# Two-layer decoder trunk on one core: causal masks, priorities of head operations, and the place of two slab sums

## The chip, the cores and the metric

The kernel runs on one core of a Trainium2 chip. The core has four computing engines with a queue of instructions each: TensorE (PE; its weight loads are shown apart as PEld), VectorE (DVE), ScalarE (ACT) and GpSimd (POOL). SyncE (SP) issues the transfers. Each engine works through its queue in order; an instruction that has to wait for another engine, by a semaphore, holds everything behind it in the queue. The metric is the device time of one execution in microseconds, lower is better.

## The reference

The input is 256 tokens of width 2048, a memory of 256 tokens, and the weights. There are two layers, all in float32:

```python
for i in range(DEPTH):
    if i == 1: sk1, sk2, sv = shared_kv(x, kv_norm, w_kv, k_norm, cos, sin)
    u = rms_norm(x, mix_norm[i]) @ w_in[i]
    # layer 0: causal pooling of 4 channel groups, then a linear map per group
    # layer 1: 12 difference heads, a = softmax(q1 k1) - lam * softmax(q2 k2), causal,
    #          o = a @ v, then an RMS norm per head
    # both: 4 memory heads, softmax(q k_mem) @ v_mem, not causal
    x = x + concat([token_out, mem_out]) @ w_out[i]
    x = x + squared_relu_mlp(rms_norm(x, ffn_norm[i]), w_ff1[i], w_ff2[i])
```

The causal mask adds -1e30 to the scores of later keys ahead of the softmax.

## The kernel before

**Precision and weights.** Each float32 weight is split into a high part in TensorE's fast float32 format and a low part. ScalarE makes the high part (`hi`, L157), VectorE the low part (`lo`, L158), both into a ring of six slots of 512 columns. Transfers by SP bring the weights in 512 KB pieces (`raw`, and `slab` for the part described last). One slot feeds six to twelve matmuls, and the splits run three slots ahead of use (class `Feed`).

**Stages of layer 1.** The stage that the change touches is layer 1's attention. `b_tile` makes the query projections in three column blocks c = 0, 1, 2, of four heads each. After each block the queries are normed, rotated and turned (`query_rows`, `rope`, `query_scale`, `turn_queries`). Then four tiles `mq1` make the memory queries (`c_tile`), and then output tiles `wo` follow (`out_tiles`): the first three tiles are begun with the channels that are ready (eight, then four, then the last four), and tiles 3 to 15 are done one by one. Heads are not computed where they stand in the program: `at(lag, fn)` puts their parts into a table, and each completed weight slot (`tick`) runs the parts that are due. So the parts of heads are spread between the large matmuls.

**A difference head** (`diff_head`, L1175 and after) has four parts. `scores`: matmuls of both maps for the second half of the queries (`s1`, 256 keys) and for the first half (`s0`, 128 keys); the mask; a maximum over keys (L1207); four exponentials with sums (L1211); reciprocal and combination. `turn`: three transposes (`dt`, L1226) and a copy. `pv`: three output matmuls (`do`, L1232 to L1234), their squares (L1242), a reciprocal root from ScalarE and VectorE steps (`rsqrt_cols`), and two scalings into `osb` (L1250). `back`: two transposes (`o_t`, L1255) and the split into `cat1` (`split_gain`).

Two ways of masking exist. With `by_pe` false VectorE adds the mask to the scores (L1202, L1203). With `by_pe` true TensorE adds it as a bf16 matmul of the identity with the mask (L1189, L1193), and in `pv` the output is first copied out of its bank into `osb` (L1237), from which squares and scalings then read. The caller passes `c == 2`: heads 8 to 11 take the second way.

**A memory head** (`mem_head`) has scores (`ms`, L573), a maximum (L575), exponentials (L579), a reciprocal and two multiplications (L584, L586); four transposes (`mt`, L592) and a copy (L595); two output products (`mo`, L600) with a copy and a subtraction out of the bank (L601, L602). `mem_query` makes the norm of its query beforehand (`st_mq`, L553).

**PSUM.** The pool has tags with few buffers, one bank each: `mm` three (tiles `mq1`, `wo`), `s` two (`s1`, `s0`, `ms` in turn), `t` one (`dt`, `mt`, `tq`), `o` one (`do`, `mo`), `st` one (`o_t`, `st_mq`). A tile's first matmul waits until every reader of the buffer's earlier tile is done.

**What sets the order.** The program only states the work. A scheduler puts each engine's instructions in order by a priority (the earlier in the program, the higher) and by when it expects them to be ready. That order is then fixed.

**Slabs.** In the feed-forward part, half of the second weight goes through a 2x2 block scheme with seven products, whose weights are sums of blocks ("slabs"). `Feed._prepare` with job "K" makes the first two sums on VectorE (L182 and L183). `out_tiles` adds each finished output tile to the residual in two steps (`resid_add`, L638 and L639); a `wo` tile waits until the tile three before it has been added.

Of the kernel before, what the change touches and what calls it, by code (L numbers as in the profile page):

```python
# [10 lines left out]
F32 = mybir.dt.float32  # L11
# [94 lines left out]
class Feed:  # L106


    def __init__(self, nc, wst, wpool, rows, plan, dry):
        self.nc, self.wst, self.wpool, self.rows = nc, wst, wpool, rows  # L110
        self.plan, self.dry = plan, dry
        self.pos = 0
        self.slab_no = 0
        self.lp = self.pp = 0
        self.raw = {}
        self.split = {}
        self.t1 = None
        if not dry:
            self.hi = wpool.tile([P, SLOTS * 512], F32R, name="hi_ring")
            self.lo = wpool.tile([P, SLOTS * 512], F32R, name="lo_ring")  # L120
            self.busy = [False] * SLOTS
            self.at = 0
# [39 lines left out]
    def _prepare(self, p):  # L162
        sub, add = self.nc.vector.tensor_sub, self.nc.vector.tensor_add
        self.load(self.plan.need[p] + 1 + LOADS)
        if p[0] == "N":
            r = ("N", p[1] // 2)
            c = p[1] % 2 * 512
            if not self._split(p, self.raw[r][:, c : c + 512], 1):
                return False
            if c:  # L170
                del self.raw[r]
            return True
        ra, rb = self.raw[("S", p[1], 0)], self.raw.get(("S", p[1], 1))
        t1 = self.t1[1 if p[1] % 32 > 28 else p[1] % 2]

        def both():
            t2 = rb[:, 0:512].unsqueeze(1).to_broadcast([P, 2, 512])
            two = ra.rearrange("p (a c) -> p a c", a=2)
            sub(two, t2, two)

        if p[0] in "KL":
            add(t1, ra[:, 0:512], rb[:, 0:512])  # L182
            sub(rb[:, 0:512], t1, rb[:, 512:1024])  # L183
            if p[0] == "L":
                both()
# [77 lines left out]
def program(ctx, tc, plan, dry, xT, memT, par, lam, cst, wst, yT):  # L263
# [8 lines left out]
    feed = Feed(nc, wst, wp, tp, plan, dry)  # L272

    acc = {}

# [12 lines left out]
    def flush():  # L288
        while pend:
            tick()  # L290


    def vt(name):
        return tp.tile([P, T], F32, tag="v", bufs=6, name=name)
# [246 lines left out]
    def mem_query(src, gq, cols):  # L541
# [1 line left out]

        q = vt("mq")
        sq = vt("mq_sq")
        nc.scalar.activation(q, src, AF.Copy, scale=gq)
        nc.scalar.activation(sq, src, AF.Square)
        y = tp.tile([P, 2], F32, tag="m2", bufs=12, name="mq_y")

        def stats():  # L550
            st = stat("st_mq")
            for t in range(2):
                nc.tensor.matmul(  # L553
                    st[:, 2 * t : 2 * t + 2], sq[:, t * P : t * P + P], ones_h,
                    start=True, stop=True,
                )
            v2 = tp.tile([P, 2], F32, tag="m2", bufs=12, name="mq_v")
            nc.vector.tensor_mul(v2, st[:, 0:4].rearrange("p (a b) -> p a b", b=2)[:, :, 0], cols[1])
            nc.vector.tensor_scalar_add(v2, v2, EPS)
            rsqrt_cols(y, v2)  # L560
            nc.vector.tensor_mul(y, y, cols[0])

        at(2, stats)
        return q, y
# [1 line left out]
    def mem_head(q, y, k, v, e, pT, out, lag, pv_lag=6):  # L566
# [3 lines left out]
        def scores():  # L570
            s = pp.tile([P, 2, T], F32, tag="s", bufs=2, name="ms")
            for t in range(2):
                nc.tensor.matmul(s[:, t, :], q[:, t * P : t * P + P], k, start=True, stop=True)  # L573
            m = tp.tile([P, 2], F32, tag="m2", bufs=12, name="mm_max")
            nc.vector.tensor_reduce(out=m, in_=s, axis=AX.X, op=ALU.max, negate=True)  # L575
            nc.vector.tensor_mul(m, m, y)
            z = tp.tile([P, 2], F32, tag="m2", bufs=12, name="mm_sum")
            for t in range(2):
                nc.scalar.activation(  # L579
                    e[:, t, :], s[:, t, :], AF.Exp, bias=m[:, t : t + 1], scale=y[:, t : t + 1],  # L580
                    accum_out=z[:, t : t + 1],
                )
            zr = tp.tile([P, 2], F32, tag="m2", bufs=12, name="mm_rec")
            nc.vector.reciprocal(zr, z)  # L584
            for t in range(2):
                nc.vector.tensor_scalar_mul(e[:, t, :], e[:, t, :], zr[:, t : t + 1])  # L586

        def turn():
            t4 = pp.tile([P, 2, T], F32, tag="t", bufs=1, name="mt")
            for mb in range(2):  # L590
                for t in range(2):
                    nc.tensor.transpose(  # L592
                        t4[:, mb, t * P : t * P + P], e[:, t, mb * P : mb * P + P], ident
                    )
            nc.scalar.copy(pT, t4)  # L595

        def pv():
            o = pp.tile([P, T], F32, tag="o", bufs=1, name="mo")
            for mb in range(2):
                nc.tensor.matmul(o, v(mb), pT[:, mb, :], start=mb == 0, stop=mb == 1)  # L600
            nc.scalar.copy(out[:, 0:T], o)  # L601
            nc.vector.tensor_sub(out[:, T : 2 * T], o, out[:, 0:T].bitcast(F32))  # L602

        at(lag, scores)
        at(lag + 4, turn)
# [30 lines left out]

    def resid_add(ps, n):
        nc.vector.tensor_add(resid[:, n, :], resid[:, n, :], ps[:, 0:T])  # L638
        nc.vector.tensor_add(resid[:, n, :], resid[:, n, :], ps[:, T : 2 * T])  # L639

    def resid_done(n, splits, square=True):
        for dst, g in splits:
# [385 lines left out]
    def out_tiles(l, cat, lead, ks, fx, between):  # L1028
# [6 lines left out]
        for n in range(NK):  # L1035
# [3 lines left out]
            else:  # L1039
                ps = mmt("wo")  # L1040
                a_part(ps, "w_out", l, n, sum(lead, []) + ks, cat)
            resid_add(ps, n)
            resid_done(n, [(fx, G_FFN + 16 * l)])

    group_u(3)
# [109 lines left out]
    def turn_queries(rows, i, pair):  # L1155
# [4 lines left out]
                    t4[:, c, t * P : t * P + P], rows[:, t, (i + c) * P : (i + c) * P + P], ident  # L1160
                )
        for g, r in enumerate((slice(0, 64), slice(64, 128))):
            nc.scalar.activation(pair[g][r], t4[r], AF.Copy, scale=qcol[r])


    gsub = cp.tile([P, 1], F32, name="gsub")
# [8 lines left out]
    def diff_head(h, q, y, lag, pv_lag, back_lag, by_pe):  # L1175
# [6 lines left out]
        def scores():  # L1182
# [11 lines left out]
            else:  # L1194
# [9 lines left out]
            mx = tp.tile([P, 2, 2], F32, tag="m4", bufs=6, name="mx")  # L1204
            z = tp.tile([P, 2, 2], F32, tag="m4", bufs=6, name="z")
            for t, s in ((1, s1), (0, s0)):
                nc.vector.tensor_reduce(out=mx[:, t, :], in_=s, axis=AX.X, op=ALU.max, negate=True)  # L1207
            nc.vector.tensor_mul(mx, mx, yh)
            for t, s, e in ((1, s1, e1), (0, s0, e0)):
                for m in range(2):  # L1210
                    nc.scalar.activation(  # L1211
                        e[:, m, :], s[:, m, :], AF.Exp, bias=mx[:, t, m : m + 1],
                        scale=yh[:, t, m : m + 1], accum_out=z[:, t, m : m + 1],
                    )

            zr = tp.tile([P, 2], F32, tag="m2", bufs=12, name="zr")
            nc.vector.reciprocal(zr, z[:, :, 1])
            stt(zr, zr, nlam, z[:, :, 0], ALU.mult, ALU.mult)
            stt(ez, z[:, :, 0], EPS, z[:, :, 0], ALU.mult, ALU.mult)
            for t, e, dst in ((1, e1, a[:, P : P + T]), (0, e0, a[:, 0:P])):  # L1220
                stt(dst, e[:, 1, :], zr[:, t : t + 1], e[:, 0, :], ALU.mult, ALU.add)

        def turn():
            t3 = pp.tile([P, 384], F32, tag="t", bufs=1, name="dt")
            for i in range(3):
                nc.tensor.transpose(t3[:, i * P : i * P + P], a[:, i * P : i * P + P], ident)  # L1226
            nc.scalar.copy(aT, t3)

        def pv():
            o = pp.tile([P, 2, P], F32, tag="o", bufs=1, name="do")  # L1230
# [1 line left out]
            nc.tensor.matmul(o[:, 0, :], aT[:, 0:P], vv[:, 0, hs], start=True, stop=True)  # L1232
            nc.tensor.matmul(o[:, 1, :], aT[:, P:T], vv[:, 0, hs], start=True, stop=False)
            nc.tensor.matmul(o[:, 1, :], aT[:, T : T + P], vv[:, 1, hs], start=False, stop=True)  # L1234
            osb = vt("osb").rearrange("p (a b) -> p a b", a=2)
            if by_pe:
                nc.vector.tensor_copy(osb, o)  # L1237
                o = osb
            ss = tp.tile([P, 2], F32, tag="m2", bufs=12, name="o_ss")
            junk = vt("o_sq")  # L1240
            for t in range(2):
                nc.scalar.activation(  # L1242
                    junk[:, t * P : t * P + P], o[:, t, :], AF.Square, accum_out=ss[:, t : t + 1]
                )
            v = tp.tile([P, 2], F32, tag="m2", bufs=12, name="o_v")
            stt(v, ss, 1.0 / P, ez, ALU.mult, ALU.add)
            yo = tp.tile([P, 2], F32, tag="m2", bufs=12, name="o_y")
            rsqrt_cols(yo, v)
            for t in range(2):
                nc.vector.tensor_scalar_mul(osb[:, t, :], o[:, t, :], yo[:, t : t + 1])  # L1250

            def back():
                f = pp.tile([P, T], F32, tag="st", bufs=1, name="o_t")
                for t in range(2):
                    nc.tensor.transpose(f[:, t * P : t * P + P], osb[:, t, :], ident)  # L1255
                split_gain(cat1[:, h, :], f, gsub)

            at(back_lag, back)

# [4 lines left out]
    for c in range(3):  # L1264
        ps = pair_of_banks(0, "q1")
        b_tile(ps, "w_in_q", 1, c, x_mx)
        rows, v = query_rows(ps, c1, 64)
        rope(rows, qtab)
        y = query_scale(v, c1)
        for i in range(2):  # L1270
            j = 2 * c + i
            q = qb[j % 3]
# [104 lines left out]
```

## Time and profile before

| What | Value |
| --- | --- |
| median of three runs | 2045.28 us (2045.19 to 2045.52) |
| the profiled execution | 2044.93 us |
| its span | 2043.1 us |
| PE busy | 2037.2 us |
| DVE busy | 1716.2 us |
| ACT busy | 1349.8 us |
| POOL busy | 51.9 us |
| DMA | 390.75 MB, mean 191 GB/s |

The span runs from the first to the last instruction of the program; the execution's own time is 1.8 us longer. The granted TensorE clock is 1.0 throughout. Matmuls are pipelined, so that the duration of one (0.39 us for 512 columns) is longer than the distance to the next (0.23 us): a gap shows as a distance above the usual one, or as idle time in brackets. In the timeline, "x2" merges neighbours of one line; in the list of waits the columns are the total, the number, and the longest, in us.

### The profile page before, as it was taken

The page shows a single profiled execution, that of the slowest core. Times are in us where ns is not written, and L with a number is a line of the kernel's source. Part 1 is how long each engine was busy: PE and PEld are TensorE (multiplying, and loading weights), DVE is VectorE, ACT ScalarE, POOL GpSimd, SP SyncE. Part 2 cuts the span into 40 slices and gives each one's busy share as a digit, 9 for nine tenths or more (in the row PEclk, how much of TensorE's full clock was granted, in tenths as well). Part 3 has the DMA queues.
Part 4 walks back from the last instruction along what each step waited for, and adds up shares of the span by engine and source line. Part 5 has one row for each costly group of instructions (what it writes and reads, how often), then busy time and mean ns, then how long its engine had stood idle before and what let it go on. Part 6 is the DMA issues. An engine that isn't in the chain of part 4 may idle for free.

```text
span 2043.1 us, 32257 instructions
## 1 busy us (share of the span) xinstructions
PE 2037.2 (100%) x11060; PEld 1755.3 (86%) x11060; DVE 1716.2 (84%) x3215; ACT 1349.8 (66%) x2505; POOL 51.9 (3%) x67
## 2 busy tenths in 40 slices
PE   9999999999999999999999999999999999999999
PEld 8888888888888888888888888888888888888888
DVE  8888889889879978999766687889879978988997
ACT  7765566666666756768665697566657666666764
POOL 0001200000000000000000000310000000000000
PEclk9999999999999999999999999999999999999999
DMA  9556556555555555655565543656555555565564
GB/s 314 178 181 190 188 174 206 197 196 197 186 201 202 189 207 191 207 169 182 194 228 186 170 140 103 196 166 207 196 196 205 186 196 196 186 210 195 196 209 135
DMA packets 110470, 390.75 MB, mean 191 GB/s; under 512 B 12256, under 2 KB 14944, under 8 KB 110304
## 3 DMA queue, kind: packets, MB, share of 16 engines
q1 hardware_dynamic: 110160, 388.59, 57.1%
q8 instruction: 86, 1.41, 0.3%
q14 instruction: 80, 0.66, 0.1%
q10 hardware_dynamic: 144, 0.10, 0.0%
HBM read 386.54 MB, written 2.10 MB: 190 GB/s over the span
## 4 chain that ended last, share of the span: by engine, by line
PE 99%; ACT 1%; DVE 1%; issue 0%
PE x_bank L391 33%; PE x_bank L393 16%; PE wo L391 6%; PE p L746 5%; PE p L747 5%; PE p L748 5%; PE wo L393 3%; PE u L391 2%; PE ff L391 2%; PE u L393 1%; PE k L417 1%; PE k L419 1%; PE v L417 1%; PE k L418 1%; PE v L419 1%; PE v L418 1%
## 5 line engine op out<-in xcount | busy, mean ns | idle before, releaser
L157 ACT CAST hi_ring<-raw 128x512 fp32r<-128x512 f32 x1193 | 736.7, 620 | 529.5 <-PE x_bank L391 308.0
L158 DVE TENSOR_TENSOR lo_ring<-raw,hi_ring 128x512 fp32r<-128x512 f32 x1193 | 817.2, 695 | 206.7 <-ACT hi_ring L157 165.5
L391 PE MATMUL x_bank<-fx,hi_ring 128*128 128x512 f32 x1920 | 602.1, 395 | 0.0
L393 PEld LDWEIGHTS x_bank<-fx,lo_ring 128*128 128x128 f32 x1920 | 361.0, 188 | 83.6
L393 PE MATMUL x_bank<-fx,lo_ring 128*128 128x256 f32 x1920 | 377.4, 278 | 0.0
L391 PEld LDWEIGHTS x_bank<-fx,hi_ring 128*128 128x128 f32 x1920 | 301.4, 189 | 9.3
L391 PE MATMUL x_bank<-z,hi_ring 128*128 128x512 f32 x960 | 301.1, 395 | 0.0
L158 DVE TENSOR_TENSOR lo_ring<-slab,hi_ring 128x1024 fp32r<-128x1024 f32 x188 | 230.1, 1224 | 54.3 <-ACT hi_ring L157 53.6
L157 ACT CAST hi_ring<-slab 128x1024 fp32r<-128x1024 f32 x188 | 196.9, 1047 | 73.1 <-PE x_bank L391 36.2
L393 PEld LDWEIGHTS x_bank<-z,lo_ring 128*128 128x128 f32 x960 | 180.5, 188 | 41.7
L393 PE MATMUL x_bank<-z,lo_ring 128*128 128x256 f32 x960 | 188.8, 278 | 0.0
L391 PE MATMUL wo<-cat,hi_ring 128*128 128x512 f32 x512 | 162.5, 398 | 0.5 <-DVE resid L639 0.5
L391 PEld LDWEIGHTS x_bank<-z,hi_ring 128*128 128x128 f32 x960 | 151.9, 189 | 6.5 <-ACT room L672 0.4
L393 PEld LDWEIGHTS wo<-cat,lo_ring 128*128 128x128 f32 x512 | 95.9, 188 | 21.7
L672 ACT COPY room<-x_bank 128x512 f32<-128x512 f32 x180 | 104.9, 583 | 2.0 <-PE x_bank L393 2.0
L393 PE MATMUL wo<-cat,lo_ring 128*128 128x256 f32 x512 | 101.4, 279 | 0.0
L746 PE MATMUL p<-hi_ring,sit 128*128 128x512 f32 x256 | 100.5, 393 | 0.0
L747 PE MATMUL p<-hi_ring,sit 128*128 128x512 f32 x256 | 100.2, 391 | 0.0
L748 PE MATMUL p<-lo_ring,sit 128*128 128x512 f32 x256 | 99.7, 389 | 0.0
L391 PEld LDWEIGHTS wo<-cat,hi_ring 128*128 128x128 f32 x512 | 79.1, 189 | 2.2 <-PE wo L393 0.9
L717 ACT ACTIVATE room<-room 128x256 f32<-128x256 f32 x128 | 53.2, 416 | 39.1 <-DVE room L300 39.1
L746 PE MATMUL p<-hi_ring,z 128*128 128x512 f32 x192 | 75.2, 392 | 0.0
(313 smaller groups left out, 3102.3 us busy)
## 6 DMA issues: line engine op xcount, KB each, us to landing
raw<-in_w SPq DMA_DIRECT2D x595, 512.0 KB, 4.0
slab<-in_w SPq DMA_DIRECT2D x124, 512.0 KB, 3.3
resid<-in_x SPq DMA_DIRECT2D x8, 256.0 KB, 5.9
room<-in_w SPq DMA_DIRECT2D x4, 512.0 KB, 4.2
memraw<-in_mem SPq DMA_DIRECT2D x4, 512.0 KB, 3.6
out_y<-resid SPq DMA_DIRECT2D x16, 128.0 KB, 1.8
memraw<-in_mem SPq DMA_DIRECT2D x7, 256.0 KB, 6.3
raw<-in_w SPq DMA_DIRECT2D x3, 256.0 KB, 3.5
```

The lines of the kernel that those rows point to most:

```text
L157: self.nc.scalar.copy(hi, src)
L158: self.nc.vector.tensor_sub(lo, src, hi.bitcast(F32))
L391: nc.tensor.matmul(ps, hi, xs[:, k, :], start=first and c == 0, stop=False)
L393: nc.tensor.matmul(ps[:, T : 2 * T], lo, xs[:, k, 0:T], start=False, stop=last and c == len(ks) - 1,)
L417: nc.tensor.matmul(ps[t], xl, hi, start=k == 0, stop=False)
L418: nc.tensor.matmul(ps[t], xh, hi, start=False, stop=False)
L419: nc.tensor.matmul(ps[t], xh, lo, start=False, stop=k == NK - 1)
L672: nc.scalar.copy(x, ps)
L717: at(3, lambda: nc.scalar.activation(stage[i % 8], y[:, 0:T], AF.Square))
L746: nc.tensor.matmul(ps, a[1], hi, start=first, stop=False)
L747: nc.tensor.matmul(ps, a[0], hi, start=False, stop=False)
L748: nc.tensor.matmul(ps, a[0], lo, start=False, stop=last)
```

## The change

Three things. First, `diff_head` is called with `by_pe` False for all heads: heads 8 to 11 now take VectorE's masks, and the output is no longer copied out of its bank. Second, most ScalarE and VectorE operations of the heads, of `mem_query`, of the queries' norm and turning, stand in `with early():`, which is the scheduler's context of high priority. Third, an ordering edge, without a semaphore, for the scheduler alone: the first slab sum after output tile 2 (the third of the 16) is put behind that tile's second residual addition; the program sets it once in each layer.

```diff
-            add(t1, ra[:, 0:512], rb[:, 0:512])
+            one = add(t1, ra[:, 0:512], rb[:, 0:512])
+            if self.gate:
+                self.tc.add_manual_dep(
+                    one.ins, self.gate,
+                    mybir.DependencyInfo(
+                        mybir.DependencyClass.NoSync, mybir.DependencyReason.SCHED_ONLY
+                    ),
+                )
+                self.gate = None
...
+    def early():
+        return tc.high_priority()
...
-        nc.scalar.activation(q, src, AF.Copy, scale=gq)
-        nc.scalar.activation(sq, src, AF.Square)
+        with early():
+            nc.scalar.activation(q, src, AF.Copy, scale=gq)
+            nc.scalar.activation(sq, src, AF.Square)
...
-            nc.scalar.copy(out[:, 0:T], o)
-            nc.vector.tensor_sub(out[:, T : 2 * T], o, out[:, 0:T].bitcast(F32))
+            with early():
+                nc.scalar.copy(out[:, 0:T], o)
+                nc.vector.tensor_sub(out[:, T : 2 * T], o, out[:, 0:T].bitcast(F32))
...
-            resid_add(ps, n)
+            done = resid_add(ps, n)
+            if n == 2 and not dry:
+                feed.gate = done.ins.name
...
-                nc.vector.tensor_add(s1[:, :, P:T], s1[:, :, P:T], mask)
-                nc.vector.tensor_add(s0, s0, mask)
+                with early():
+                    nc.vector.tensor_add(s1[:, :, P:T], s1[:, :, P:T], mask)
+                    nc.vector.tensor_add(s0, s0, mask)
...
-                    2 * j + g, q[g], y, *((6 + 4 * h, 8, 4 if c == 0 else 3) if c < 2 else (6 + 2 * h, 6, 3)), c == 2
+                    2 * j + g, q[g], y, *((6 + 4 * h, 8, 4 if c == 0 else 3) if c < 2 else (6 + 2 * h, 6, 3)), False
```

In the same way the following stand in the context of high priority: the rest of `scores`, the copy in `turn` and all of `pv` and `back` of a difference head but the matmuls; the statistics of `mem_query`; softmax and copies of a memory head; `query_rows`, `rope` and `query_scale` of layer 1, and the copies of `turn_queries`. The lags of all parts are as before.

More of the change, by code (lines that the diff above doesn't have):

```diff
@@ L106, with __init__ @@
 class Feed:
-    def __init__(self, nc, wst, wpool, rows, plan, dry):
-        self.nc, self.wst, self.wpool, self.rows = nc, wst, wpool, rows
+    def __init__(self, tc, wst, wpool, rows, plan, dry):
+        self.tc, self.nc, self.wst, self.wpool, self.rows = tc, tc.nc, wst, wpool, rows
         self.plan, self.dry = plan, dry
@@ L181, in _prepare @@
         if p[0] in "KL":
-            add(t1, ra[:, 0:512], rb[:, 0:512])
+            one = add(t1, ra[:, 0:512], rb[:, 0:512])
[6 more added lines that the diff above has]
+                )
+                self.gate = None
             sub(rb[:, 0:512], t1, rb[:, 512:1024])
@@ L271, in program @@
     nc.scalar.preload_act_table_set("natural_log_exp_and_others")
-    feed = Feed(nc, wst, wp, tp, plan, dry)
+    feed = Feed(tc, wst, wp, tp, plan, dry)
     acc = {}
@@ L556, in stats @@
                 )
[L557 to L561, printed above, removed]
+            with early():
+                v2 = tp.tile([P, 2], F32, tag="m2", bufs=12, name="mq_v")
+                nc.vector.tensor_mul(v2, st[:, 0:4].rearrange("p (a b) -> p a b", b=2)[:, :, 0], cols[1])
+                nc.vector.tensor_scalar_add(v2, v2, EPS)
+                rsqrt_cols(y, v2)
+                nc.vector.tensor_mul(y, y, cols[0])
         at(2, stats)
@@ L573, in scores @@
                 nc.tensor.matmul(s[:, t, :], q[:, t * P : t * P + P], k, start=True, stop=True)
[L574 to L586, printed above, removed]
+            with early():
+                m = tp.tile([P, 2], F32, tag="m2", bufs=12, name="mm_max")
+                nc.vector.tensor_reduce(out=m, in_=s, axis=AX.X, op=ALU.max, negate=True)
+                nc.vector.tensor_mul(m, m, y)
+                z = tp.tile([P, 2], F32, tag="m2", bufs=12, name="mm_sum")
+                for t in range(2):
+                    nc.scalar.activation(
+                        e[:, t, :], s[:, t, :], AF.Exp, bias=m[:, t : t + 1], scale=y[:, t : t + 1],
+                        accum_out=z[:, t : t + 1],
+                    )
+                zr = tp.tile([P, 2], F32, tag="m2", bufs=12, name="mm_rec")
+                nc.vector.reciprocal(zr, z)
+                for t in range(2):
+                    nc.vector.tensor_scalar_mul(e[:, t, :], e[:, t, :], zr[:, t : t + 1])
         def turn():
@@ L594, in turn @@
                     )
-            nc.scalar.copy(pT, t4)
+            with early():
+                nc.scalar.copy(pT, t4)
         def pv():
@@ L600, in pv @@
                 nc.tensor.matmul(o, v(mb), pT[:, mb, :], start=mb == 0, stop=mb == 1)
-            nc.scalar.copy(out[:, 0:T], o)
-            nc.vector.tensor_sub(out[:, T : 2 * T], o, out[:, 0:T].bitcast(F32))
+            with early():
+                nc.scalar.copy(out[:, 0:T], o)
+                nc.vector.tensor_sub(out[:, T : 2 * T], o, out[:, 0:T].bitcast(F32))
         at(lag, scores)
@@ L638, in resid_add @@
         nc.vector.tensor_add(resid[:, n, :], resid[:, n, :], ps[:, 0:T])
-        nc.vector.tensor_add(resid[:, n, :], resid[:, n, :], ps[:, T : 2 * T])
+        return nc.vector.tensor_add(resid[:, n, :], resid[:, n, :], ps[:, T : 2 * T])
     def resid_done(n, splits, square=True):
@@ L1162, in turn_queries @@
         for g, r in enumerate((slice(0, 64), slice(64, 128))):
-            nc.scalar.activation(pair[g][r], t4[r], AF.Copy, scale=qcol[r])
+            with early():
+                nc.scalar.activation(pair[g][r], t4[r], AF.Copy, scale=qcol[r])
     gsub = cp.tile([P, 1], F32, name="gsub")
@@ L1201, in scores @@
                 mask = const[:, C_MASK : C_MASK + P].unsqueeze(1).to_broadcast([P, 2, P])
-                nc.vector.tensor_add(s1[:, :, P:T], s1[:, :, P:T], mask)
-                nc.vector.tensor_add(s0, s0, mask)
[L1204 to L1218, printed above, removed]
@@ L1219, in scores @@
-            stt(ez, z[:, :, 0], EPS, z[:, :, 0], ALU.mult, ALU.mult)
-            for t, e, dst in ((1, e1, a[:, P : P + T]), (0, e0, a[:, 0:P])):
-                stt(dst, e[:, 1, :], zr[:, t : t + 1], e[:, 0, :], ALU.mult, ALU.add)
+                with early():
+                    nc.vector.tensor_add(s1[:, :, P:T], s1[:, :, P:T], mask)
+                    nc.vector.tensor_add(s0, s0, mask)
+            with early():
+                mx = tp.tile([P, 2, 2], F32, tag="m4", bufs=6, name="mx")
+                z = tp.tile([P, 2, 2], F32, tag="m4", bufs=6, name="z")
+                for t, s in ((1, s1), (0, s0)):
+                    nc.vector.tensor_reduce(out=mx[:, t, :], in_=s, axis=AX.X, op=ALU.max, negate=True)
+                nc.vector.tensor_mul(mx, mx, yh)
+                for t, s, e in ((1, s1, e1), (0, s0, e0)):
+                    for m in range(2):
+                        nc.scalar.activation(
+                            e[:, m, :], s[:, m, :], AF.Exp, bias=mx[:, t, m : m + 1],
+                            scale=yh[:, t, m : m + 1], accum_out=z[:, t, m : m + 1],
+                        )
+                zr = tp.tile([P, 2], F32, tag="m2", bufs=12, name="zr")
+                nc.vector.reciprocal(zr, z[:, :, 1])
+                stt(zr, zr, nlam, z[:, :, 0], ALU.mult, ALU.mult)
+                stt(ez, z[:, :, 0], EPS, z[:, :, 0], ALU.mult, ALU.mult)
+                for t, e, dst in ((1, e1, a[:, P : P + T]), (0, e0, a[:, 0:P])):
+                    stt(dst, e[:, 1, :], zr[:, t : t + 1], e[:, 0, :], ALU.mult, ALU.add)
@@ L1226, in turn @@
                 nc.tensor.transpose(t3[:, i * P : i * P + P], a[:, i * P : i * P + P], ident)
-            nc.scalar.copy(aT, t3)
+            with early():
+                nc.scalar.copy(aT, t3)
         def pv():
@@ L1234, in pv @@
             nc.tensor.matmul(o[:, 1, :], aT[:, T : T + P], vv[:, 1, hs], start=False, stop=True)
[L1235 to L1250, printed above, removed]
+            with early():
+                osb = vt("osb").rearrange("p (a b) -> p a b", a=2)
+                if by_pe:
+                    nc.vector.tensor_copy(osb, o)
+                    o = osb
+                ss = tp.tile([P, 2], F32, tag="m2", bufs=12, name="o_ss")
+                junk = vt("o_sq")
+                for t in range(2):
+                    nc.scalar.activation(
+                        junk[:, t * P : t * P + P], o[:, t, :], AF.Square, accum_out=ss[:, t : t + 1]
+                    )
+                v = tp.tile([P, 2], F32, tag="m2", bufs=12, name="o_v")
+                stt(v, ss, 1.0 / P, ez, ALU.mult, ALU.add)
+                yo = tp.tile([P, 2], F32, tag="m2", bufs=12, name="o_y")
+                rsqrt_cols(yo, v)
+                for t in range(2):
+                    nc.vector.tensor_scalar_mul(osb[:, t, :], o[:, t, :], yo[:, t : t + 1])
             def back():
@@ L1255, in back @@
                     nc.tensor.transpose(f[:, t * P : t * P + P], osb[:, t, :], ident)
-                split_gain(cat1[:, h, :], f, gsub)
+                with early():
+                    split_gain(cat1[:, h, :], f, gsub)
             at(back_lag, back)
@@ L1266, in program @@
         b_tile(ps, "w_in_q", 1, c, x_mx)
-        rows, v = query_rows(ps, c1, 64)
-        rope(rows, qtab)
-        y = query_scale(v, c1)
+        with early():
+            rows, v = query_rows(ps, c1, 64)
+            rope(rows, qtab)
+            y = query_scale(v, c1)
         for i in range(2):
```

## The prediction

> **What bounds the kernel now.** I read the page first, then busy time by stage, then the stage that the diff touches in order of time. The page:
>
> ```profile
> span 2043.1 us, 32257 instructions
> ...
> PE 2037.2 (100%) x11060; PEld 1755.3 (86%) x11060; DVE 1716.2 (84%) x3215; ACT 1349.8 (66%) x2505; POOL 51.9 (3%) x67
> ...
> PE 99%; ACT 1%; DVE 1%; issue 0%
> ```
>
> TensorE is the bound and the chain of waits is TensorE for 99%. So time is gained only by taking TensorE work away or by closing its few gaps, and lost only by opening gaps. Busy time by stage; the columns are length, then PE, PEld, DVE, ACT, POOL busy, then clock and DMA:
>
> ```profile
> 1150.00:1219.00 69.00, 68.65 (x398) 59.65 (x397) 58.00 (x191) 57.30 (x169) 0.00 (x0) 1.00 0.41 132
> 1219.00:1277.00 58.00, 57.20 (x392) 51.19 (x390) 45.57 (x155) 44.97 (x146) 0.00 (x0) 1.00 0.37 118
> ```
>
> 1150 to 1277 us is the attention of layer 1; the last four difference heads (A, B, C, D: heads 8 to 11) and the four memory heads (M0 to M3) lie in the second row. VectorE and ScalarE are busy some 78% there: not full, but each is a queue in order, so a late instruction holds what stands behind it. TensorE's waits in all:
>
> ```profile
> PE warm L338 <- DVE ones_d L331: 1.0, 1, 1.0
> PE mt L592 <- DVE att L586: 0.8, 1, 0.8
> PE wo L391 <- DVE resid L639: 0.5, 2, 0.3
> ```
>
> Start by start, against the even spacing of its neighbours (0.23 us for 512 columns, 0.116 for 256, 0.109 for 128), TensorE loses about 2.2 us between 1219 and 1277 and another 2.2 between 1150 and 1219. That is all there is to win beside removed work.
>
> The resource to look at is the output bank: tag `o` has one buffer, and every head's output product `do` (L1232 to L1234) and every memory head's `mo` (L600) uses it. An early head, and then head A with M0 behind it:
>
> ```profile
> 1167.59 0.38 PE L1232 MATMUL do<-big,att 128*128 128x128 f32 x2
> 1168.45 0.28 ACT L1242 ACTIVATE o_sq<-do 128x128 f32<-128x128 f32 x1 [0.23 <-PE do L1234]
> 1171.50 0.60 DVE L1250 TENSOR_SCALAR osb<-do,o_y 128x128 f32<-128x128 f32 x2
> ...
> 1240.67 0.39 PE L1232 MATMUL do<-big,att 128*128 128x128 f32 x2
> 1242.60 0.42 DVE L1237 COPY osb<-do 128x256 f32<-128x256 f32 x1
> 1243.43 0.43 PE L600 MATMUL mo<-att,mv 128*128 128x256 f32 x1
> ```
>
> The early head holds the bank from 1167.59 to 1172.11, 4.52 us: squares, logarithm, exponential, three small VectorE steps and two scalings all lie before its release. Head A is copied out; the bank is free at 1243.02, after 2.35 us, and `mo` starts at 1243.43.
>
> **The change part by part.** The order of the instructions on each engine, compared before and after, shows nothing moved on SP or POOL, no DMA added, and differences almost only from head 6 of layer 1 to output tile 3.
>
> *Masks.* Heads A to D lose 16 bf16 matmuls (L1189, L1193). Head C's scores with masks run from 1235.57 to 1237.35, 1.78 us, of which 0.10 is a wait; head 7's without run from 1210.42 to 1211.65, 1.23. So 0.45 us a head, 1.8 us of TensorE time gone. VectorE gets eight additions (L1202, L1203) of 0.43 us, 3.4 us, on the way from scores to softmax.
>
> *The copy.* The same argument, now False, also drops the copy L1237, because both hang on `by_pe`. VectorE saves 4 x 0.42 us and pays 8 x 0.06 more for scaling from the bank (0.346 against 0.284). But heads A to D now hold the output bank up to their scalings. The holds of heads 0 to 6 in this trace, first `do` to end of second scaling, are 4.52, 7.53, 7.37, 4.52, 4.52, 7.81 and 6.45 us: mean 6.10. (Head 7's, 10.20, is left out: nothing wanted the bank until A.) Now the cover: how much TensorE work the new order puts between each head's first `do` and the next user of the bank, by the spacings above.
> - A to M0's `mo`: `do` 0.65, D's s1 0.86, two back transposes 0.22, three turns 0.33, three `wo` 0.46, D's s0 0.43, four `mt` 0.44: 3.39 us.
> - B to C's `do`: `do` 0.65, fifteen `wo` 2.52, turns 0.33, back 0.22: 3.72.
> - C to M1's `mo`: `do` 0.65, four back 0.22, eight `wo` 1.37, `mt` 0.44, half of M3's scores 0.43: 3.11.
> - D to M2's `mo`: `do` 0.65, seventeen `wo` 2.86, back 0.22: 3.73.
>
> Together 13.95 us. (M0 and M1 hold the bank 1.9 to 2.2 us here and have 2.4 and 2.3 us of work before the next head: covered.) TensorE is in order, so what is not covered is a gap: 4 x 4.52 - 13.95 = 4.1 us at the shortest hold, 4 x 6.10 - 13.95 = 10.4 at the mean, 4 x 7.81 - 13.95 = 17.3 at the longest. I take 10.4, because the new VectorE order favours long holds for two of the four: A's `o_v` stands behind the mask of D's s0, and C's stands behind the whole softmax end of M2. D's s0 in turn needs the score bank (tag `s`, two buffers) that M1's scores leave; the new order puts 3.0 us between them, while M1's kind took 4.87 us from last score matmul to last exponential at its shortest here. So 1.9 us of A's gap is certain in another way, too. B and D have only weight splits (0.7 us each) in their way and may come near 4.5.
>
> [...]
>
> *Priority.* Head operations move ahead of weight splits on ScalarE and VectorE. Splits have slack: ScalarE waits for ring slots (L157 on x_bank alone 347.4 us in all). I price it at nothing by itself, from -2.2 (all small gaps of 1150 to 1219 close) to +2 (a few splits late by 0.7 us each); its effect on the holds is in the bounds above.
>
> *The ordering edge.* In layer 1 the two slab sums (L182, L183) now run at 1257.39 and 1258.11, 1.2 us on VectorE ahead of M2's maximum, and M2's `mt` later waits 0.76 us (0.92 by its spacing). They move behind the sum of output tile 2. That takes away this gap and about 0.2 beside it: -1.1, between 0 and -1.2. The waits of tile 3 on L639 (0.5 us, both layers) stay: between L638 and L639 stands a weight split, in the old order and in the new one.
>
> Sum: +10.4 - 1.8 - 1.1 = +7.5 us. Against the profiled execution's 2044.93 us (span 2043.1 and 1.8 around it) that is 2052.4; the median shown, 2045.28, is 0.35 higher, so 2052.8.
>
> **The rivals.**
> - *Priority keeps the holds short* (no change, or a little faster). This is the other side. With the mean hold h the change costs 4h - 13.95 - 2.9 us: nothing at h = 4.21, and under 0.2% (4.1 us) up to h = 5.24. For it: three of seven holds are 4.52, and head operations now come first. Against it: the shortest holds occur where neighbours are two weight tiles apart, not where four difference and four memory heads meet. At 4.52 each the time is 2045.28 + 4.1 - 2.9 = 2046.5.
> - *Everything covered* (faster). All gaps go: -1.8 - 4.4 - 0.5 = -6.7, 2038.6. It needs h of 3.5; adding the steps of the early head without its queueing, 0.65 + 3.40 = 4.05, already exceeds that. Partly covered, it is 2041.
> - *Longer still.* If softmax of M1 to M3 also slips (each `mt` waits as M2's did, 0.9 us) and holds come near 7.8, it is 2045.28 + 17.3 + 2.7 - 2.9 = 2062.
> - *The ordering edge does nothing*, since the waits on L639 stay: +1.1 on my sum, 2053.9, inside my range.
>
> **How the numbers follow.** 0.2% (4.1 us) is about what a measurement of this kernel can tell from no change. My own case with the longer one: 0.77, with 2052.8 the likeliest, and 2049 to 2060 its own range. Short holds: 0.16. Faster: 0.07, near 2040. The range leaves out the faster case, the lower part of the short holds and the far end of the longer one: 2046.0 to 2059.5. Faster 0.07, same 0.16, slower 0.77.
>
> **What would show it.** In the profile after, `mo` (L600's line) and `do` should appear among what TensorE waits for, released by the scalings (L1250's line); TensorE's busy share between the first mask of head A and output tile 3 should fall by some 8 us of gaps, and that stretch, 58 us now, take 64 to 67. No 128x128 bf16 matmul should be left, and VectorE should show 24 mask additions in place of 16. Slab sums of layer 1 should follow the residual sums. I am wrong if the holds of heads A to D average under 5.2 us, or if the gaps are there but released by weight splits.

## The result, and the profile after

The changed kernel takes 2056.25 us (median of 5, 2055.89 to 2061.11) against 2045.23 us for the kernel before beside it: +11.0 us, a ratio of 1.0058 with a 95% interval of 1.0045 to 1.007. The profiled execution took 2056.06 us, 11.1 more than the one before. The first part of its page:

```profile
span 2054.3 us, 32233 instructions
...
PE 2040.4 (99%) x11044; PEld 1753.6 (85%) x11044; DVE 1717.2 (84%) x3219; ACT 1348.8 (66%) x2505; POOL 52.3 (3%) x67
...
PE 97%; ACT 2%; DVE 1%; DMA 0%; issue 0%; SPq 0%
```

TensorE has 16 instructions less (the mask matmuls) and VectorE as much to do as before, yet TensorE's share of the chain falls from 99% to 97%, and ScalarE's rises from 1% to 2%. Busy time by stage of the same execution, with the columns of the table before (length, then PE, PEld, DVE, ACT, POOL busy, clock, DMA):

```profile
1150.00:1219.00 69.00, 68.70 (x397) 59.56 (x396) 57.64 (x189) 57.02 (x169) 0.00 (x0) 1.00 0.43 138
1219.00:1277.00 58.00, 51.18 (x325) 44.22 (x323) 39.42 (x138) 39.14 (x128) 0.00 (x0) 0.94 0.27 89
1277.00:1289.00 12.00, 10.66 (x57) 8.47 (x57) 8.72 (x27) 7.57 (x19) 0.49 (x1) 1.00 0.44 139
```

Up to 1219 nothing changed. Then TensorE is busy 51.18 of 58 us where it was 57.20, with 325 instructions where it had 392, at a mean clock of 0.94; VectorE and ScalarE fall to some 68%, too, so no engine became the bound by its load. What TensorE waited for, over the whole execution (total, times, longest, in us):

```profile
PE wo L405 <- DVE cat L314: 2.5, 3, 1.2
PE mo L618 <- DVE osb L1276: 1.7, 2, 1.5
PE s L1222 <- ACT att L596: 1.6, 1, 1.6
...
PE wo L405 <- DVE resid L658: 0.9, 2, 0.7
PE mt L609 <- DVE att L603: 0.9, 1, 0.9
```

Before, this list held 0.8 for `mt` and 0.5 for the residual sum. Now the largest is `wo` behind the split of a head's output into `cat1`; the output bank (`mo` behind the scalings) comes second, the score bank (D's `s0` behind M1's exponentials) third.

To compare kernels I use one number, the stall: over all starts of TensorE from 1219 to 1295 us, the distance to the next start less the even spacing of that shape. It is 3.85 us before and 16.31 after. (It counts every small excess, so it stands above the prediction's 2.2 us for the gaps up to 1277.) The difference, 12.46, less 1.8 for the removed matmuls, is 10.7; the rest of the program adds some 0.4.

### The profile page after: what moved, and what is told of

Same layout as the page of the kernel before. It is cut to its first block, busy times and chain, and to the rows that moved or that the text cites. A ratio compares the mean times of both kernels' runs of the same rounds, so it can differ in the third digit from the quotient of the medians.

```text
span 2054.3 us, 32233 instructions
## 1 busy us (share of the span) xinstructions
PE 2040.4 (99%) x11044; PEld 1753.6 (85%) x11044; DVE 1717.2 (84%) x3219; ACT 1348.8 (66%) x2505; POOL 52.3 (3%) x67
## 4 chain that ended last, share of the span: by engine, by line
PE 97%; ACT 2%; DVE 1%; DMA 0%; issue 0%; SPq 0%
PE x_bank L405 33%; PE x_bank L407 16%; PE wo L405 5%; PE p L765 5%; PE p L766 5%; PE p L767 5%; PE wo L407 3%; PE u L405 2%; PE ff L405 2%; PE u L407 1%; PE k L431 1%; PE k L433 1%; PE v L433 1%; PE k L432 1%; PE v L431 1%; PE v L432 1%
```

## The experiments

Each kernel was timed in rounds with the kernel before; "against before" is the difference of the medians. The holds of the trace suggested at first that the bank was the cause, as predicted, so the first four runs were to tell that from late softmax and from priority. In some runs of the slower kernels TensorE's mean granted clock is 0.996 to 0.999 (the traces at the end show 0.50 for some us), and in every run of the kernel before it is 1.000; so the last column gives the difference for the runs at full clock alone (mean clock 1.000), with their number.

| kernel | median, us | against before | stall, us | at full clock (runs) |
| --- | --- | --- | --- | --- |
| the change | 2056.25 | +11.0 | 16.31 | none of 5 |
| copy kept | 2053.29 | +7.6 | 11.54 | +5.9 (2 of 5) |
| last argument alone (masks and copy) | 2050.36 | +4.7 | 10.56 | +4.6 (8 of 11) |
| priority and edge | 2048.89 | +3.2 | 8.71 | +3.0 (8 of 11) |
| two halves of the bank | 2056.68 | +11.0 | 16.7 | none of 5 |
| masks alone | 2048.62 | +3.2 | 6.95 | +1.6 (5 of 11) |
| copy alone | 2049.71 | +4.2 | 7.87 | +4.0 (9 of 11) |
| priority alone | 2051.75 | +6.3 | 9.73 | +5.1 (1 of 6) |
| edge alone | 2046.09 | +0.6 | 4.57 | +0.6 (11 of 11) |
| edge, priority by 40 places | 2045.95 | +0.6 | 4.50 | +0.6 (11 of 11) |
| edge, priority for outputs alone | 2046.71 | +1.4 | 4.87 | +1.4 (11 of 11) |
| masks alone, no additions | 2044.29 | -1.0 | 4.43 | -1.0 (11 of 11) |
| the change, twelve transposes more | 2055.62 | +10.3 | 14.58 | none of 5 |

The stall is that of the profiled execution, the median that of 5 to 11 runs; where the clock fell in some runs and not in others they differ by up to 2 us.

### Copy kept, with the rest of the change

```diff
-                if by_pe:
+                if h >= 8:
                     nc.vector.tensor_copy(osb, o)
```

> The changed kernel, but heads A to D copy their output out of the bank again; masks by VectorE, priority and ordering edge stay. Theory (output bank): a hold ends with the copy, some 2.4 us after the first output product, under the cover of 3.1 to 3.7 us, so the gaps between those heads go and the half clock with them: 2042 to 2047 us. Rival (the mask additions and the new VectorE order make the softmax late, whatever the bank does): most of the 11 us stays, 2052 to 2056.

It took 2053.29 us (ratio 1.0038, 1.0025 to 1.005): in the rival's range. The wait of `mo` on the scalings is gone, but others stand in its place:

```profile
PE do L1257 <- DVE cat L621: 1.2, 1, 1.2
...
PE wo L405 <- DVE cat L314: 1.0, 2, 0.6
PE do L1257 <- DVE rc L376: 0.9, 1, 0.9
...
PE mt L609 <- DVE att L603: 0.9, 1, 0.9
PE o_t L1281 <- DVE cat L314: 0.9, 1, 0.9
```

So the dropped copy carries 3.4 of the 11.0 us (each against its own runs of before) when the rest of the change is there, not all of it; and part of the 3.4 is the clock, which fell in every run of the change (means of 0.996 to 0.998) and not in two of these five (1.000). The theory that the bank is the whole cause fell here.

### The last argument alone

```diff
-  ... (6 + 2 * h, 6, 3)), c == 2
+  ... (6 + 2 * h, 6, 3)), False
```

> The kernel before with nothing changed but the last argument of heads A to D (masks by VectorE and no copy); no priority, no ordering edge. Theory (output bank): the same holds of 4 to 9 us against some 14 us of cover, so most of the loss is here without the rest of the change: 2052 to 2058 us. Rival (priority lengthens the holds): 2045 to 2048.

2050.36 us (1.0027, 1.0018 to 1.0036): between the two. Masks and copy together are less than half of the loss, so priority or the edge must cost something beside them.

### Priority and edge, without the last argument

```diff
-  ... (6 + 2 * h, 6, 3)), False
+  ... (6 + 2 * h, 6, 3)), c == 2
```

> The changed kernel with masks by TensorE and the copy as before: priority and ordering edge alone. Theory (output bank): no loss; the gap at M2's back transposes (1 us) goes: 2043.5 to 2046 us. Rival (priority is what costs): 2050 or more.

2048.89 us (1.0018, 1.001 to 1.0027): neither range held it, but the sign is the rival's. What I had priced at -1.1 together costs 3.2.

### Two halves of the output bank

```diff
+    def out_half():
+        if not turns:
+            halves.append(pp.tile([P, 2, T], F32, tag="o", bufs=1, name="oo"))
+        turns.append(0)
+        return halves[0][:, len(turns) % 2, :]
...
-            o = pp.tile([P, 2, P], F32, tag="o", bufs=1, name="do")
+            o = out_half().rearrange("p (a b) -> p a b", a=2)    # heads 8 to 11; M0 to M3 likewise
```

> The changed kernel, but heads A to D and M0 to M3 take turns in two halves of the output bank, so that a product waits for the hold before the last and not for the last one. Theory (output bank): the waits on the scalings go (A to M0, C to M1: about 3.5 to 9 us with the half clock); D's wait for the score bank (1.7 us) and the wait on the split of a head (1.3 us) can stay: 2044 to 2051 us. Rival (late softmax whatever the bank does): 2054 to 2057.

2056.68 us, as the change. But the trace shows that the edit did not do what it was to do:

```profile
PE oo L622 <- DVE osb L1290: 1.9, 2, 1.7
```

The product of a memory head still waits for the scalings of the difference head in the other half; the two halves are one buffer to whatever sets the waits. The run tells nothing of the bank.

### The four parts one by one

Masks alone: the last argument False and the copy tied to `h >= 8`. Copy alone: `if by_pe:` ahead of the copy replaced by `if False:`. Priority alone and edge alone: the changed kernel with the other parts put back.

> The kernel before, with the masks of heads A to D added by VectorE and the copy out of the output bank kept; no priority, no ordering edge. First theory (the dropped copy is what costs): the sixteen matmuls go and nothing else is lost, 2043 to 2046 us. Second theory, formed after the runs with the copy kept (2053.3) and with the last argument alone (2050.4): the mask additions make every softmax later, and TensorE, which has only some 14 us of output projection to put between the heads, waits for the softmax and for the splits of the heads: 2048 to 2051 us.

> The kernel before, with the copy out of the output bank dropped and the masks left on TensorE; no priority, no ordering edge. First theory (the dropped copy is what costs): holds of 4 to 8 us as in the changed kernel, 2050 to 2056 us. Second theory (late softmax): the bank alone costs little, 2045 to 2048 us.

> The kernel before with the heads' priority alone. First theory: nothing, 2044.5 to 2046.5 us. Second theory (priority puts weight splits behind the heads' operations and changes the order in which TensorE gets output projection and heads): it carries the 3.2 us of priority and edge together, and the gap at M2's back transposes stays: 2048 to 2051 us.

> The kernel before with the ordering edge alone. First theory: the gap of 1 us at M2's back transposes goes, 2044 to 2045.5 us. Rival (the slab sums or the splits behind them come late instead, and tile 3 waits longer than 0.4 us for the residual sum): 2045.5 to 2048 us.

Masks alone 2048.62 us (1.0014, 1.0005 to 1.0023), copy alone 2049.71 (1.0022, 1.0013 to 1.003), priority alone 2051.75 (1.0029, 1.0018 to 1.0041), edge alone 2046.09 (1.0003, 0.9994 to 1.0011). Three of the four parts make the kernel slower by themselves, and priority, which I had priced at nothing, most of all, somewhat above the range of the second theory. For the copy neither range held: its price lies between my two theories. Half of the price of the masks is the clock, which fell in six of their eleven runs (means of 0.998 and 0.999): at full clock it is 1.6 us. So the copy on top of the masks, 1.5 us by the medians (4.7 less 3.2), is 3.0 at full clock (4.6 less 1.6), near its price alone. In the trace of the copy alone the bank itself shows for 0.2 us: M0's `mo` starts 0.20 us after A's scalings end, but that is at 1250.63, 7.2 us later than before, and most of the loss surfaces behind it, at a split (1.4) and an `mt` (0.7). The sum of the four, 14.3 us, is more than the 11.0 of all together, which fits parts that fill the same waits. TensorE's waits with masks alone, then with priority alone, then with the edge alone:

```profile
PE wo L391 <- DVE cat L300: 1.6, 1, 1.6
...
PE mt L592 <- DVE att L586: 0.7, 1, 0.7
```

```profile
PE mt L609 <- DVE att L603: 2.0, 1, 2.0
PE wo L405 <- DVE cat L314: 1.1, 2, 0.8
```

```profile
PE o_t L1281 <- DVE rc L375: 0.7, 1, 0.7
PE wo L405 <- DVE resid L658: 0.7, 2, 0.5
PE wo L405 <- DVE cat L314: 0.4, 1, 0.4
```

The edge does take away M2's `mt` wait (0.8 before), but back transposes, a split and the residual sum come late in its stead: 1.8 us in this list where there were 1.3.

### What the parts have in common

All the slow kernels but the copy alone have the same thing late. Head 7, the last before A, was never copied out, in any kernel here, and A's first `do` needs its bank. In the timeline before (ScalarE and VectorE; A's `do` is at 1240.67, shown above):

```profile
1234.32 0.56 ACT L1211 ACTIVATE att<-s,mx,qy 128x256 f32<-128x256 f32 x1
...
1236.75 0.30 ACT L1242 ACTIVATE o_sq<-do 128x128 f32<-128x128 f32 x1
...
1239.76 0.61 DVE L1250 TENSOR_SCALAR osb<-do,o_y 128x128 f32<-128x128 f32 x2
```

and in the changed kernel (ScalarE, VectorE, TensorE):

```profile
1233.17 0.62 ACT L158 CAST hi_ring<-raw 128x512 fp32r<-128x512 f32 x1 [1.31 <-PE mq L420]
1234.60 0.62 ACT L158 CAST hi_ring<-raw 128x512 fp32r<-128x512 f32 x1 [0.81 <-PE mq L420]
...
1237.84 0.59 ACT L613 COPY att<-mt 128x512 f32<-128x512 f32 x1 [1.01 <-PE mt L609]
...
1239.20 0.56 ACT L1235 ACTIVATE att<-s,mx,qy 128x256 f32<-128x256 f32 x1
...
1241.67 0.29 ACT L1268 ACTIVATE o_sq<-do 128x128 f32<-128x128 f32 x1
...
1245.70 0.61 DVE L1276 TENSOR_SCALAR osb<-do,o_y 128x128 f32<-128x128 f32 x2
...
1246.47 0.38 PE L1257 MATMUL do<-big,att 128*128 128x128 f32 x2
```

Head 7's product starts at 1230.2 in both. Its squares stand on ScalarE behind the exponentials of head B, and ScalarE stands idle (the numbers in brackets) while they could run. B's exponentials need B's `s0`, which needs the score bank that M0's exponentials leave, which need M0's maximum, which stands on VectorE behind the softmax of A. The times of this chain:

| | before | edge, 40 places | masks alone | priority alone | copy kept | the change |
| --- | --- | --- | --- | --- | --- | --- |
| head 7's first `do` | 1230.17 | 1230.66 | 1229.98 | 1230.91 | 1230.81 | 1230.18 |
| A's second maximum | 1221.96 | 1222.45 | 1222.84 | 1223.09 | 1224.87 | 1224.24 |
| M0's maximum | 1228.78 | 1229.26 | 1229.34 | 1231.09 | 1233.17 | 1232.54 |
| M0's exponentials | 1230.78 | 1231.26 | 1230.59 | 1232.55 | 1235.76 | 1235.12 |
| B's first `s0` | 1232.34 | 1232.83 | 1232.27 | 1234.39 | 1237.01 | 1236.38 |
| head 7's squares | 1236.75 | 1237.24 | 1237.33 | 1238.61 | 1242.31 | 1241.67 |
| head 7's bank free | 1240.37 | 1240.86 | 1242.48 | 1242.81 | 1246.95 | 1246.31 |
| A's first `do` | 1240.67 | 1241.15 | 1242.95 | 1242.96 | 1247.11 | 1246.47 |
| stall | 3.85 | 4.50 | 6.95 | 9.73 | 11.54 | 16.31 |

The first row shows how far TensorE itself is behind at head 7; with 40 places every row is some 0.5 us later, and nothing more. From the second row on, each row waits for the one above it, or stands behind it in a queue. With masks alone the chain starts further down: B's `s0` is not late, and of the 2.1 us by which the bank comes free later, 1.5 lie between head 7's squares and scalings, where VectorE has an addition, a maximum and two weight splits more to do first. In all kernels of the study A's `do` starts 0.15 to 0.5 us after head 7's bank is free. Among those that keep the copy, the stall is under 5 us where A's `do` starts before 1241.6, 6.95 to 9.73 where it starts between 1242.9 and 1243.4, and 11.54 at 1247.1. TensorE does not idle at once: it goes on to the output projection, which in the changed kernel starts when 28.0 us of TensorE work is left up to the last `mo`, against 20.2 before. That work is then missing between the heads: after D's `do` 9.6 us of it are left where there were 16.2. The five kernels with 15.9 us or more there (before, edge alone, 40 places, outputs alone, no additions) all stall under 5 us; those with 14.6 or less, all the others, stall 6.95 to 16.7.

That head 7's bank is the link is read from these rows; no kernel that copies head 7 out was run, so it is not shown by an edit. The copy alone costs 4 us with A's `do` at 1241.47, so it is not the only way to lose time.

### What it is in priority and in the masks

Priority by 40 places:

```diff
-        return tc.high_priority()
+        return tc.high_priority(40)
```

> Priority and ordering edge as in the kernel of these two, but the heads' operations are moved ahead by 40 places instead of to the very front, so that they keep their order among each other. If priority costs time because at the front all the heads' blocks are equal and lose their order among each other (TensorE then gets the head steps late and the output projection early): as the edge alone, 2045.5 to 2046.5 us. If any preference of heads over weight splits costs: 2048 to 2050.

2045.95 us (1.0003, 0.9994 to 1.0012), as the edge alone. So a small step forward costs nothing, and the move to the very front does. But the small step also changes little: from 1150 to 1300 us 9 of 378 VectorE and 6 of 334 ScalarE instructions stand in another order than with the edge alone, against 132 and 86 with priority to the front. Whether the front costs because the heads lose their order among each other, or because any strong preference of heads over weight splits does, stays open; the first is my reading, not shown.

Priority for the output chain of a head alone:

> Ordering edge, and priority for the output chain of a head alone (squares to scalings and the split after the back transposes), not for softmax and not for the memory heads; masks by TensorE and the copy as before. If what costs is the softmax of later heads that comes ahead of the outputs of earlier ones, putting the outputs first takes away the waits that the edge alone left at the back transposes and at the split (1.1 us): 2044.5 to 2045.5 us. If any priority costs: 2047 to 2050.

2046.71 us (1.0007, 0.9998 to 1.0015): in neither range. The waits at the back transposes (0.7) and at the split (0.4) are still there, head 7's hold is 10.07 us (10.20 before), and the residual wait is 0.7. Putting outputs first gains nothing here, though it does reorder (64 and 28 instructions).

Masks alone without the eight additions, so that heads 8 to 11 get no causal mask at all:

```diff
-                nc.vector.tensor_add(s1[:, :, P:T], s1[:, :, P:T], mask)
-                nc.vector.tensor_add(s0, s0, mask)
+                if h < 8:
+                    nc.vector.tensor_add(s1[:, :, P:T], s1[:, :, P:T], mask)
+                    nc.vector.tensor_add(s0, s0, mask)
```

> As the kernel with VectorE masks alone (2048.6 us), but heads A to D get no mask at all: the eight additions are left out, and the masks of these four heads with them. If the additions on the path from scores to softmax are what costs there, the time falls below that of the kernel before by about the 1.8 us of matmuls: 2043 to 2045 us. If it is the other order of the queues that costs: 2046 to 2049.

2044.29 us (0.9995, 0.9987 to 1.0004), 4.3 us less than with the additions, 2.8 less than with them at full clock: eight additions of 0.43 us, 3.4 us of VectorE time, cost 2.8 us and, in half of the runs, the fall of the clock, though VectorE has idle time in the stage (with the additions it is busy 53.67 of the 66.00 us from 1219 to 1285). Without them the removed matmuls bring 1.0 us, not 1.8, and that is within the interval.

### Filling a gap

```diff
-                for t in range(2):
+                for t in [0, 1] + mb * extra * [1]:    # extra = 12 for M1
                     nc.tensor.transpose(
```

> The changed kernel with twelve needless transposes of 0.109 us each more on TensorE, in the gap after M1's back transposes; nothing else is moved. The profile shows the clock at 0.50 from some 1253.6 to 1260 us, worth about 2.2 us. If idle TensorE causes that, 1.3 us less of idling shortens it or takes it away, and the time falls although there is more work: 2053.5 to 2055.5 us. If the clock has another cause, or the idling that is left is enough: 2056 to 2057.5.

2055.62 us, 2053.79 to 2057.91: both ranges have runs in them. In the profiled execution the clock had already fallen at 1251.1, ahead of the filled gap, so the edit came too late to tell; its clock rows stand in the last section. No version beat the kernel before by more than its interval.

## Why the prediction was right, and where it was wrong

The forecast, 2052.8 us and slower, was right in sign; 2056.25 lies in the range, 3.4 above the forecast. That the size came out is luck: run alone, no part has the size that the sum gave it, and the copy's share, too large, stood in for what masks and priority cost.

**The place** was right: but for 0.4 us all of the loss lies between 1219 and 1289. Of what was to show it, 24 mask additions, no bf16 matmul, slab sums behind the residual sums (first at 1295.59, after 1288.26) and `mo` behind the scalings are there; `do` behind the scalings is not in the list of waits. The stretch from A's first score to the end of tile 2's sums grew from 57.5 to 68.3 us, more than the 64 to 67.

**The copy** (+10.4). The arithmetic of the holds held: 8.78, 4.34, 6.68 and 3.97 us, mean 5.94 against 6.10; the work in between was 3.40, 3.73, 3.12 and 3.75 us as counted; and TensorE lost 10.07 us in these four stretches. The bank does end each of them: the next product starts 0.05 to 0.14 us after the last scaling. But kept copies take away 3.4 of 11.0 us, and the dropped copy alone costs 4.2. The step that failed is the one from where a wait shows to what causes it: of the 5.4 us between A and M0's `mo`, 1.8 were the output bank; 1.7 were M1's score bank (the prediction had named it, at 1.9) and 1.4 head 7's split, late by the chain above (the brackets are TensorE's idle time):

```profile
1249.90 0.50 PE L405 MATMUL wo<-cat,hi_ring 128*128 128x512 f32 x1 [1.19 <-DVE cat L314]
...
1252.21 0.71 PE L1222 MATMUL s<-big,att 128*128 128x128 f32 x4 [1.57 <-ACT att L596]
...
1255.31 0.80 PE L618 MATMUL mo<-att,mv 128*128 128x256 f32 x1 [1.48 <-DVE osb L1276]
```

With the copy kept, most of the stall was still there, at other steps. And the sentence on head 7, left out because "nothing wanted the bank until A", passed over the hold that mattered: A wanted it, 0.30 us after its release even before.

**The masks** (-1.8) cost +3.2 alone, +1.6 at full clock. The prediction put 3.4 us of additions "on the way from scores to softmax" and gave that way no price; it is 4.3 us, 2.8 at full clock, against 1.0 for the matmuls.

**Priority** (nothing, from -2.2 to +2) costs +6.3 alone, outside its bounds. They were made from weight splits that come late. The trace of before could not show what the front of the queue does to the order of the heads among each other; the comparison of the orders could, since it has the output projection start earlier, and I read only covers from it.

**The edge** (-1.1) is +0.6, within noise: its rival, that it does nothing, was nearest. The wait at `mt` went, three others came. With priority it is worth more: priority alone costs 6.3 us, with the edge 3.2, and an `mt` that waits 2.0 us there waits 0.7 with it.

**Not in the sum at all**: the fall of the clock, some 2.4 us: the work from M0's `mo` to B's `do`, 2.4 us at even spacing, took 4.8 at a clock of 0.50.

**The rivals.** Short holds: out, since the mean hold is over 5.24. Longer still: `mt` waited 0.9 as it said, but the holds averaged 5.94, not 7.8, and the time stayed under its 2062. With the copy alone dropped, head A held the bank 8.96 us where it was 2.35, at +4.2 us. By VectorE's own time alone the copy, 0.42 us of VectorE a head, 1.7 in all, does not pay, yet it saves 4.0 us alone and 3.0 on top of the masks at full clock, which I put down to the bank that comes free.

## What to carry to other kernels

When several engines hand small steps to each other, price an addition by what stands behind it in its queue and follow that chain to the engine that bounds, also across units that the change does not touch. A wait that TensorE shows is where lateness surfaces; only taking the suspected cause away tells whether the time goes or surfaces at the next step. A priority that puts many like steps at the very front can cost more than it brings: here it cost 6.3 us alone, while a step of 40 places changed little in the order and nothing in the time. And look at the clock of each run before pricing a part by medians: the clock fell in some runs of a kernel and not in others, and made half of what the masks seemed to cost (1.6 of 3.2 us).

## What the runs showed of the hardware

In the profiled executions of five kernels TensorE's granted clock fell to 0.50 after a stretch in which TensorE was only some half busy (48 to 53% below), without idling through it. The stretch of 3.41 us before the fall, and the half clock, in the changed kernel, then with priority and edge, then with twelve transposes more (busy time, clock by stretch):

```profile
1249.83:1253.24 3.41, 1.76 (x10) 1.32 (x11) 2.62 (x10) 2.24 (x9) 0.00 (x0) 1.00 0.35 137
1253.24:1260.08 6.84, 5.36 (x16) 4.23 (x16) 3.59 (x15) 4.09 (x14) 0.00 (x0) 0.50 0.00 0
```

```profile
1261.37:1264.78 3.41, 1.64 (x9) 1.15 (x9) 2.10 (x9) 2.33 (x10) 0.00 (x0) 1.00 0.31 120
1264.78:1268.20 3.42, 3.42 (x14) 2.97 (x14) 1.44 (x7) 1.91 (x10) 0.00 (x0) 0.50 0.00 0
```

```profile
1247.70:1251.12 3.42, 1.64 (x10) 1.08 (x8) 3.07 (x10) 1.64 (x4) 0.00 (x0) 1.00 0.49 155
1251.12:1258.02 6.90, 5.92 (x24) 5.65 (x25) 3.63 (x14) 4.23 (x18) 0.00 (x0) 0.51 0.01 3
```

TensorE was busy 48 to 52% in these stretches; the longest pause in that of the changed kernel is 1.57 us (ahead of `s`, shown above). With two halves it was busy 2.13 of the 4.00 us from 1250 to 1254, with priority alone 1.97 of the 4.00 us from 1262 to 1266 (the fall is at their end: a mean clock of 0.90 from 1264 to 1266), and the clock of the next 2 us was 0.51 and 0.50. In the changed kernel the clock stayed at 0.50 for 6.84 us, and TensorE was busy 1.94 of the first 3.42 and all of the second; with priority and edge for 3.42 us, with TensorE busy throughout.

With masks and copy together, a stretch as little busy passed at full clock in the profiled execution:

```profile
1249.27:1252.68 3.41, 1.69 (x9) 1.09 (x7) 2.66 (x11) 3.23 (x12) 0.00 (x0) 1.00 0.45 154
```

That is 50% busy, where 52% in the changed kernel was followed by the fall: the busy time of the profile, in which the ends of matmuls are modelled, does not tell the two apart. The same program gives two sets of times: masks and copy ran nine times at 2050.07 to 2050.92 us at mean clocks of 1.000 or 0.999, and twice at 2054.11 and 2054.58 at 0.997 and 0.998. What decides between the two is not shown.
